# Norms of a two-block transformer: sums folded on VectorE, small steps moved there, columns spread by transposes, and the first four projections issued in a fixed order

## The chip, the cores and the metric

One NeuronCore of a Trainium2 chip runs the whole program. The metric is the device time of one execution in microseconds, given as the median of several executions. TensorE multiplies (its weight loads are listed apart, as PEld), VectorE (DVE) and ScalarE (ACT) work elementwise, GpSimd (POOL) does small steps, and SyncE (SP) issues the transfers.

## What is computed

The input is 256 tokens of 1024 features in float32. A first block has two layers (a retention and sparse-attention mixer, then a gated recurrent mixer, each followed by a gated feed-forward layer with 2816 inner features) with root-mean-square norms ahead of every part. A second block follows with a differential-attention layer and a chunked-attention layer, each again with a feed-forward layer, and here a layer norm stands *behind* every part:

```python
def layer_norm(x, g, b):
    mu = jnp.mean(xf, axis=-1, keepdims=True)
    var = jnp.mean(jnp.square(xf - mu), axis=-1, keepdims=True)
    y = (xf - mu) * lax.rsqrt(var + LN_EPS) * g + b
...
    x = layer_norm(DEEPNORM_ALPHA * x + mix, ln_g[l, 0], ln_b[l, 0])
    x = layer_norm(DEEPNORM_ALPHA * x + swiglu_2(x, ...), ln_g[l, 1], ln_b[l, 1])
```

There are thus five root-mean-square norms (four in the first block, one at its end) and four layer norms, the last of which ends the program.

## The kernel before, in words

Activations lie feature-major: 1024 features are eight slices of 128 partitions by 256 tokens, kept in four pair tiles (`State`). Every projection multiplies in three passes to keep float32 precision: both the weights and the activations are split into a high part on ScalarE and a low part on VectorE (`weights`, L235; `split`, L292), and `mm3` (L246) issues high by high, high by low and low by high for each of eight slices. One projection of 128 outputs, a *product* below, is thus 24 matmuls. Weights come by SyncE's queue, 512 KB at a time.

**The sums of a norm** run over partitions, so TensorE does them: `Stats` (L307) adds up squares (and, for a layer norm, the values too) over slices on VectorE and then multiplies each remaining 128 by 256 part by a constant column (L333). In the kernel before, slices 0 to 5 are folded into one part (`upto=4`) and slices 6 and 7 go to TensorE as they are: three parts, two token halves each, six matmuls a sum. The first norm of the program folds all eight (`upto=6`, L684). A float32 matmul shows in the profile as two records, so six matmuls are twelve records.

**The small steps** turn two sums per token into the reciprocal root. A layer norm copies the sums out of PSUM on VectorE (L507) and does five steps on GpSimd (L509, L510, L346, L349, L513). A root-mean-square norm does a copy on VectorE (L361) and two steps on GpSimd (L348, L349). `spread` (L352) then multiplies a broadcast column by the identity (L355), so that each token's number stands on all 128 partitions, and one copy takes that out of PSUM (L366 on VectorE, L517 on ScalarE).

**A layer norm defers its division.** `Norm` (L482) computes z = ALPHA times the earlier stream plus the mixer's output (L490), scales it by the gain on ScalarE (L493), splits it (L295, L296) and lets the next projections run on the result before the norm is known: `project` (L534) issues a product into a PSUM bank and only then, on VectorE, corrects it by the spread reciprocal root and mean (L541, L543, L544). Norm 0 stands behind the first attention layer's output projection, Norm 1 behind the first feed-forward layer, Norm 2 behind the second attention layer, and `last_norm` (L547) behind the last feed-forward layer. Behind Norm 0 and Norm 2 the first four products may use four banks (three of `pa`, one of `tr`); behind Norm 1 only the three of `pa`.

**The order of the work** is set by a planner at build time. It simulates the engines and, on each engine, takes what is ready, the earlier in the program first. What it decides is then each engine's fixed order. An order-only edge (`tc.issue_after(x)`) puts what follows behind instruction `x` on the same engine's queue, without waiting for `x` to finish.

Of the kernel before, what the change touches and what calls it, by code (L numbers as in the profile page):

```python
# [16 lines left out]
S = 256  # L17
# [151 lines left out]
def _model(es, tc, I, out):  # L169
# [12 lines left out]
    class State:  # L182
        def __init__(self):
            self.t = [None] * 4
# [61 lines left out]
    def mm3(ps, hi, lo, k, h, first, last):  # L246
        a, b = hi[:, k * 128:k * 128 + 128], lo[:, k * 128:k * 128 + 128]
        T.matmul(ps, a, h[0], start=first, stop=False, skip_group_check=True)  # L248
        T.matmul(ps, a, h[1], start=False, stop=False, skip_group_check=True)  # L249
        T.matmul(ps, b, h[0], start=False, stop=last, skip_group_check=True)  # L250

# [55 lines left out]
    class Stats:  # L307
        def __init__(self, cols, tag, upto=4):
            self.cols, self.tag, self.upto, self.ps = cols, tag, upto, None
            self.first, self.acc, self.parts = {}, {}, [[] for c in cols]  # L310

        def add(self, i, src, d, n):
            if d == 0:
                self.first[i] = src
            elif d == 2:
                self.acc[i] = sp.tile([128, 2, S], F32, tag="acc", name="acc")
                V.tensor_tensor(out=self.acc[i], in0=self.first[i], in1=src, op=ALU.add)
            elif d <= self.upto:
                a = self.acc[i]
                V.tensor_tensor(out=a, in0=a, in1=src, op=ALU.add)  # L320
                if d == self.upto:
                    V.tensor_tensor(out=a[:, 0], in0=a[:, 0], in1=a[:, 1], op=ALU.add)
                    self.parts[i].append(a[:, 0])
            else:
                self.parts[i] += [src[:, j] for j in range(n)]

        def total(self, i, last=True):
            start = self.ps is None
            if start:
                self.ps = att(self.tag, (128, 2 * len(self.cols)))  # L330
            for k, p in enumerate(self.parts[i]):
                for t in range(2):
                    T.matmul(self.ps[:, 2 * i + t:2 * i + t + 1], p[:, t * 128:t * 128 + 128], self.cols[i],  # L333
                             start=start and k + t == 0, stop=last and k == len(self.parts[i]) - 1,
                             skip_group_check=True)
            self.parts[i] = []

    def square(src, n):
# [4 lines left out]
    def rpow(v, n, eps, floor=False):  # L343
        r = sp.tile([128, n], F32, tag="rp", name="rp", bufs=6)
        if floor:
            G.tensor_scalar(out=r, in0=v, scalar1=0.0, scalar2=eps, op0=ALU.max, op1=ALU.add)  # L346
        else:
            G.tensor_scalar(out=r, in0=v, scalar1=eps, scalar2=None, op0=ALU.add)  # L348
        G.tensor_tensor(out=r, in0=r, in1=mhalf[:, :n], op=ALU.pow)  # L349
        return r  # L350

    def spread(cols, ps):  # L352
        for i, c in enumerate(cols):
            for t in range(2):
                T.matmul(ps[:, i, t * 128:t * 128 + 128], c[:, t:t + 1].to_broadcast([128, 128]), ident,  # L355
                         start=True, stop=True)

    def rms_stats(stats, eps=1e-6):
        stats.total(0)
        v = sp.tile([128, 2], F32, tag="v2", name="v2", bufs=6)  # L360
        V.tensor_copy(v, stats.ps)  # L361
        rt = rpow(v, 2, eps)
        pb = att("po", (128, 1, S))
        spread([rt], pb)
        rb = sp.tile([128, S], F32, tag="rb", name="rb", bufs=2)
        V.tensor_copy(rb, pb[:, 0])  # L366
        return rb, rt

    def prep(X, goff, upto=4):
        stats, H = Stats((mcol,), "po", upto), []  # L370
        for d in range(8):
# [110 lines left out]
    class Norm:  # L482
        def __init__(self, src, gen, idx, tag, tags=()):
            self.gcol, self.bcol = V_LNG + idx * 8, V_LNB + idx * 8
            self.zg, self.HD = State(), []
            self.tags = list(tags)
# [46 lines left out]

        def project(self, w, f):  # L534
            tag, shape = self.tags.pop(0) if self.tags else "pa", [128, S + 2]
            ps = pa.tile(shape, F32, tag="pa", name="pd") if tag == "pa" else att(tag, shape)
            hi, lo = weights(w[f], 1024)
            for k in range(8):
                mm3(ps, hi, lo, k, self.HD[k], k == 0, k == 7)
            c = sp.tile([128, 2], F32, tag="dc", name="dc", bufs=4)  # L540
# [41 lines left out]
    def transpose_to(ps, src):  # L582
        T.transpose(ps, src, ident)  # L583
# [85 lines left out]
    def even_mixer(X):  # L669
# [13 lines left out]
        nc.scalar.dma_start(out=ident, in_=I["const"][:, 0:128])  # L683
        H, rb, rt = prep(X, V_MIX, 6)  # L684
        w1 = [big("w1").rearrange("p a b -> p (a b)") for i in range(4)]
# [474 lines left out]

    FOUR = ("pa", "pa", "pa", "tr")

# [4 lines left out]
    src.Y, gen = diff_mixer(X)  # L1167
    ln = Norm(src, gen, 0, "po", FOUR)
    ln = Norm(ln, ffn(ln, I["v1_0"], I["v3_0"], I["v2_0"], None), 1, 'po')

# [86 lines left out]

    ln = Norm(ln, chunk_mixer(ln), 2, "po", FOUR)
    last_norm(ln, ffn(ln, I["v1_1"], I["v3_1"], I["v2_1"], None), 3)


# [14 lines left out]
```

## Time and profile before

| | before |
|---|---|
| median of 3 runs (lowest to highest) | 1310.83 us (1310.12 to 1310.96) |
| the profiled execution: its own time | 1310.83 us |
| the profiled execution: span from first to last instruction | 1309.0 us |
| TensorE busy | 1289.9 us, 99% of the span |
| VectorE busy | 939.7 us, 72% |
| ScalarE busy | 708.2 us, 54% |
| GpSimd busy | 44.3 us, 3% |
| mean granted TensorE clock | 0.996 of full |

In the rows below, times are microseconds from the span's start. A TensorE record's length is its way through the array, and records overlap, so a stream of matmuls costs the distance from one start to the next and not the length shown. An entry in square brackets is how long the engine was idle before the instruction and what it waited for.

### The profile page before, as it was taken

The numbers are of one execution on the slowest core, as the hardware profiler recorded it, in microseconds if no ns is written. First come the engines' busy times: TensorE is split into PE (matmuls) and PEld (weight loads), VectorE is DVE, ScalarE is ACT, GpSimd is POOL, SyncE is SP. The second block draws the span as 40 slices with busy tenths as digits, with TensorE's granted clock in tenths as the row PEclk, the third lists the DMA queues.
The fourth block names the chain that finished last, engine by engine and source line by source line (L and its number), as shares of the span: only waits on it lengthen the run. The fifth ranks groups of instructions, "written<-read, shape, count | busy, mean of one in ns | idle before, by whom it ended". The sixth has DMA issues, their size and how long they took to land.

```text
span 1309.0 us, 27435 instructions
## 1 busy us (share of the span) xinstructions
PE 1289.9 (99%) x11112; PEld 1246.4 (95%) x11112; DVE 939.7 (72%) x1753; ACT 708.2 (54%) x1182; POOL 44.3 (3%) x97
## 2 busy tenths in 40 slices
PE   8999999999999999999999999999999999999997
PEld 7989999999989999999999899999999889999997
DVE  7886774645888667565678959777779757968675
ACT  6675654444644455443468856544456556554443
POOL 1000000000000000000000111000000000000000
PEclk9999999999999999999999999999999999999998
DMA  9623555554643346555555345465654544655550
GB/s 303 189 91 106 202 193 189 182 187 145 205 158 123 125 163 205 191 182 191 159 172 178 113 146 169 156 210 162 190 173 167 171 136 129 213 187 182 187 152 33
DMA packets 65358, 219.69 MB, mean 168 GB/s; under 512 B 7504, under 2 KB 7888, under 8 KB 65232
## 3 DMA queue, kind: packets, MB, share of 16 engines
q1 hardware_dynamic: 64944, 217.82, 51.1%
q8 instruction: 87, 1.43, 0.4%
q14 instruction: 39, 0.32, 0.1%
q10 hardware_dynamic: 288, 0.12, 0.0%
HBM read 216.86 MB, written 1.05 MB: 166 GB/s over the span
## 4 chain that ended last, share of the span: by engine, by line
PE 96%; DMA 1%; DVE 1%; ACT 1%; issue 0%; SPq 0%; POOL 0%; ACTq 0%; DVEq 0%
PE pa L249 13%; PE pa L248 13%; PE pa L250 13%; PE pd L249 7%; PE pd L248 7%; PE pd L250 7%; PE s L248 4%; PE s L250 4%; PE s L249 4%; PE tr L248 3%; PE tr L249 3%; PE tr L250 3%; PE pv L284 2%; PE pv L285 2%; PE pv L286 2%; PE tr L583 1%
## 5 line engine op out<-in xcount | busy, mean ns | idle before, releaser
L240 ACT ACTIVATE hi<-raw 128x1024 fp32r<-128x1024 f32 (+2 forms) x421 | 424.5, 1018 | 487.7 <-PE pa L249 166.6
L243 DVE TENSOR_TENSOR lo<-raw,hi 128x1024 fp32r<-128x1024 f32 (+2 forms) x421 | 490.7, 1173 | 251.2 <-ACT hi L240 244.6
L249 PE MATMUL pa<-hl,hi 128*128 128x256 f32 x1424 | 402.6, 284 | 0.2 <-issue 0.2
L248 PE MATMUL pa<-hh,hi 128*128 128x256 f32 x1424 | 401.0, 284 | 0.3 <-DVE x L479 0.2
L250 PE MATMUL pa<-hh,lo 128*128 128x256 f32 x1424 | 401.1, 283 | 0.0
L249 PEld LDWEIGHTS pa<-hl,hi 128*128 128x128 f32 x1424 | 268.6, 189 | 2.7 <-issue 0.9
L250 PEld LDWEIGHTS pa<-hh,lo 128*128 128x128 f32 x1424 | 268.5, 189 | 1.5 <-issue 0.5
L248 PEld LDWEIGHTS pa<-hh,hi 128*128 128x128 f32 x1424 | 267.0, 188 | 2.6 <-issue 0.5
L249 PE MATMUL pd<-hl,hi 128*128 128x258 f32 x752 | 212.7, 284 | 0.0
L250 PE MATMUL pd<-hh,lo 128*128 128x258 f32 x752 | 212.7, 283 | 0.0
L248 PE MATMUL pd<-hh,hi 128*128 128x258 f32 x752 | 211.0, 283 | 1.4 <-DVE y L543 1.4
L248 PEld LDWEIGHTS pd<-hh,hi 128*128 128x128 f32 x752 | 141.7, 190 | 1.7 <-DVE y L543 1.6
L249 PEld LDWEIGHTS pd<-hl,hi 128*128 128x128 f32 x752 | 142.5, 190 | 0.0
L250 PEld LDWEIGHTS pd<-hh,lo 128*128 128x128 f32 x752 | 142.2, 189 | 0.2
L250 PE MATMUL s<-gh,lo 128*128 128x256 f32 x352 | 97.6, 279 | 0.0
L249 PE MATMUL s<-gl,hi 128*128 128x256 f32 x352 | 97.6, 279 | 0.0
L248 PE MATMUL s<-gh,hi 128*128 128x256 f32 x352 | 95.8, 280 | 0.0
L248 PE MATMUL tr<-gh,hi 128*128 128x256 f32 x264 | 73.8, 280 | 0.0
L249 PE MATMUL tr<-gl,hi 128*128 128x256 f32 x264 | 73.7, 279 | 0.0
L250 PE MATMUL tr<-gh,lo 128*128 128x256 f32 x264 | 73.7, 279 | 0.0
L250 PEld LDWEIGHTS s<-gh,lo 128*128 128x128 f32 x352 | 66.1, 188 | 0.0
L249 PEld LDWEIGHTS s<-gl,hi 128*128 128x128 f32 x352 | 66.0, 187 | 0.0
(353 smaller groups left out, 1914.3 us busy)
## 6 DMA issues: line engine op xcount, KB each, us to landing
raw<-w SPq DMA_DIRECT2D x120, 512.0 KB, 3.8
raw<-v SPq DMA_DIRECT2D x120, 512.0 KB, 3.9
raw<-w_e SPq DMA_DIRECT2D x19, 512.0 KB, 5.8
raw<-w_aqk SPq DMA_DIRECT2D x16, 512.0 KB, 3.8
raw<-w SPq DMA_DIRECT2D x16, 384.0 KB, 3.1
raw<-v SPq DMA_DIRECT2D x16, 384.0 KB, 3.1
raw<-w_of SPq DMA_DIRECT2D x8, 512.0 KB, 3.3
raw<-w_oq SPq DMA_DIRECT2D x8, 512.0 KB, 3.9
```

The lines of the kernel that those rows point to most:

```text
L240: A.activation(hi, raw, AF.Copy)
L243: V.tensor_tensor(out=lo, in0=raw, in1=hi.bitcast(F32), op=ALU.subtract)
L248: T.matmul(ps, a, h[0], start=first, stop=False, skip_group_check=True)
L249: T.matmul(ps, a, h[1], start=False, stop=False, skip_group_check=True)
L250: T.matmul(ps, b, h[0], start=False, stop=last, skip_group_check=True)
L284: T.matmul(ps[t], xh, a, start=k == 0, stop=False)
L285: T.matmul(ps[t], xh, b, start=False, stop=False)
L286: T.matmul(ps[t], xl, a, start=False, stop=k == 7)
L583: T.transpose(ps, src, ident)
```

## The change

Sums are folded further on VectorE: the root-mean-square norms fold all eight slices, a layer norm folds all eight of its values and the first seven of its squares, and the last norm the first seven of both. The small steps except the power move from GpSimd to VectorE. `spread` uses TensorE's transpose in place of a multiplication by the identity. In a layer norm the squares are taken ahead of the gain and the split, and the first four products behind it are issued inside `Norm`: the first as it comes, the other three queued behind the last matmul of the sums, and the spread queued behind the last matmul of the third product. Behind Norm 1, too, the fourth product now uses a bank of `tr`. The core of the diff (the rest passes the new arguments on, or returns the instruction just issued):

```diff
     class Stats:
-        def __init__(self, cols, tag, upto=4):
+        def __init__(self, cols, tag, folded):
...
-            elif d <= self.upto:
+            elif d < self.folded[i]:
                 a = self.acc[i]
-                V.tensor_tensor(out=a, in0=a, in1=src, op=ALU.add)
-                if d == self.upto:
+                at = a[:, d % 2:d % 2 + n]
+                V.tensor_tensor(out=at, in0=at, in1=src, op=ALU.add)
+                if d + n == self.folded[i]:
                     V.tensor_tensor(out=a[:, 0], in0=a[:, 0], in1=a[:, 1], op=ALU.add)
                     self.parts[i].append(a[:, 0])
...
     def rpow(v, n, eps, floor=False):
         r = sp.tile([128, n], F32, tag="rp", name="rp", bufs=6)
         if floor:
-            G.tensor_scalar(out=r, in0=v, scalar1=0.0, scalar2=eps, op0=ALU.max, op1=ALU.add)
+            V.tensor_scalar(out=r, in0=v, scalar1=0.0, scalar2=eps, op0=ALU.max, op1=ALU.add)
         else:
-            G.tensor_scalar(out=r, in0=v, scalar1=eps, scalar2=None, op0=ALU.add)
+            V.tensor_scalar(out=r, in0=v, scalar1=eps, scalar2=None, op0=ALU.add)
         G.tensor_tensor(out=r, in0=r, in1=mhalf[:, :n], op=ALU.pow)
...
     def spread(cols, ps):
-                T.matmul(ps[:, i, t * 128:t * 128 + 128], c[:, t:t + 1].to_broadcast([128, 128]), ident,
-                         start=True, stop=True)
+                transpose_to(ps[:, i, t * 128:t * 128 + 128], c[:, t:t + 1].to_broadcast([128, 128]))

     def rms_stats(stats, eps=1e-6):
         stats.total(0)
-        v = sp.tile([128, 2], F32, tag="v2", name="v2", bufs=6)
-        V.tensor_copy(v, stats.ps)
-        rt = rpow(v, 2, eps)
+        rt = rpow(stats.ps, 2, eps)
...
     class Norm:
-            stats = Stats((ncol, mcol), tag)
+            stats = Stats((ncol, mcol), "po", (8, 7))
             for d, n, ps in gen:
                 z = ...
+                stats.add(1, square(z, n), d, n)
...
                 stats.add(0, z, d, n)
-                stats.add(1, square(z, n), d, n)
             stats.total(0)
-            stats.total(1)
+            summed = stats.total(1)
...
-            G.tensor_tensor(out=v, in0=st[:, 0:2], in1=st[:, 0:2], op=ALU.mult)
-            G.tensor_tensor(out=v, in0=st[:, 2:4], in1=v, op=ALU.subtract)
+            V.tensor_tensor(out=v, in0=st[:, 0:2], in1=st[:, 0:2], op=ALU.mult)
+            V.tensor_tensor(out=v, in0=st[:, 2:4], in1=v, op=ALU.subtract)
             r = rpow(v, 2, 1e-5, True)
             mr = sp.tile([128, 2], F32, tag="mr", name="mr")
-            G.tensor_tensor(out=mr, in0=st[:, 0:2], in1=r, op=ALU.mult)
-            pb = att("po", (128, 2, S))
-            spread([r, mr], pb)
+            V.tensor_tensor(out=mr, in0=st[:, 0:2], in1=r, op=ALU.mult)
+            self.ahead = {}
+            for i, (w, f, bk) in enumerate(ahead):
+                with tc.issue_after(summed.ins) if i else nullcontext():
+                    self.ahead[w.tensor.name, f] = self.product(w, f, bk)
+                if i == 2:
+                    with tc.issue_after(self.latest.ins):
+                        pb = att("po", (128, 2, S))
+                        spread([r, mr], pb)
...
     def last_norm(src, gen, idx):
-        zs, qs = Stats((ncol,), "sc"), Stats((mcol,), "sc")
+        zs, qs = Stats((ncol,), "sc", (7,)), Stats((mcol,), "sc", (7,))
...
-            if d == 4:
+            if d == 6:
                 zs.total(0, False)
                 qs.total(0, False)
...
-    ln = Norm(ln, ffn(ln, I["v1_0"], I["v3_0"], I["v2_0"], None), 1, 'po')
+    ln = Norm(ln, ffn(ln, I["v1_0"], I["v3_0"], I["v2_0"], None), 1,
+              first_four((I["w_bk"], 0), (I["w_bk"], 1), (I["w_bq"], 0), (I["w_bq"], 1)))
```

`product` is the part of `project` that issues the 24 matmuls; `project` takes a product that was issued ahead, or issues one itself.

## Rows read from the trace of the kernel before

**Rows 1.** The page: span, busy time of two engines, and the chain that ended last.

```profile
span 1309.0 us, 27435 instructions
...
PE 1289.9 (99%) x11112; PEld 1246.4 (95%) x11112; DVE 939.7 (72%) x1753; ACT 708.2 (54%) x1182; POOL 44.3 (3%) x97
...
PE 96%; DMA 1%; DVE 1%; ACT 1%; issue 0%; SPq 0%; POOL 0%; ACTq 0%; DVEq 0%
```

**Rows 2.** Waits of TensorE, longest in total first: us in total, times, longest.

```profile
PE pd L248 <- DVE y L543: 1.4, 1, 1.4
...
PE pa L355 <- POOL rp L349: 0.8, 1, 0.8
```

**Rows 3.** Whole span, instructions of L333, then of L355 alone: PE busy, records.

```profile
0.00:1309.00 1309.00, 17.19 (x148) 17.56 (x148) 1.00 0.52 168
...
0.00:1309.00 1309.00, 8.38 (x52) 7.11 (x52) 1.00 0.52 168
```

**Rows 4.** Chain that ended last, in order of time: start, us, what.

```profile
67.03 0.66 PE tr L583 x6
...
153.97 1.23 PE po L333 x12
...
799.39 0.89 PE po L355 x8
```

**Rows 5.** Timeline of TensorE behind Norm 0: start, length, line, operation.

```profile
786.93 0.52 PE L248 MATMUL pd<-hh,hi 128*128 128x258 f32 x3
...
792.96 0.50 PE L333 MATMUL po<-mcol,acc 128*128 128x1 f32 x4
793.33 1.03 PE L333 MATMUL po<-mcol,sq 128*128 128x1 f32 x8
...
802.06 0.28 PE L248 MATMUL pd<-hh,hi 128*128 128x258 f32 x1
802.18 0.28 PE L249 MATMUL pd<-hl,hi 128*128 128x258 f32 x1
```

**Rows 6.** Timeline of VectorE around Norm 0, the same columns.

```profile
788.44 0.41 DVE L490 SCALAR_TENSOR_TENSOR z<-x,s 128x256 f32<-128x256 f32 x1
788.77 0.42 DVE L322 TENSOR_TENSOR acc<-acc 128x256 f32<-128x256 f32 x1
789.11 0.69 DVE L320 TENSOR_TENSOR acc<-acc,sq 128x512 f32<-128x512 f32 x1
789.71 0.68 DVE L296 TENSOR_TENSOR hl<-x,hh 128x512 fp32r<-128x512 f32 x1
790.32 0.41 DVE L322 TENSOR_TENSOR acc<-acc 128x256 f32<-128x256 f32 x1
790.65 1.36 DVE L296 TENSOR_TENSOR hl<-x,hh 128x512 fp32r<-128x512 f32 x3
```

**Rows 7.** Timeline behind Norm 1: VectorE's last splits, TensorE's fourth product.

```profile
983.24 0.76 DVE L296 TENSOR_TENSOR hl<-x,hh 128x256 fp32r<-128x256 f32 x2
...
994.37 0.39 PE L248 MATMUL pd<-hh,hi 128*128 128x258 f32 x1 [1.36 <-DVE y L543]
```

**Rows 8.** Timeline of VectorE and GpSimd in the last norm.

```profile
1296.27 0.42 DVE L552 SCALAR_TENSOR_TENSOR x<-x,po 128x256 f32<-128x256 f32 x1 [1.16 <-PE po L250]
1298.39 0.16 DVE L562 COPY m<-s 128x2 f32<-128x2 f32 x1 [1.70 <-PE s L333]
...
1299.39 2.48 DVE L570 TENSOR_TENSOR x<-x,pa 128x512 f32<-128x512 f32 x4 [0.38 <-PE pa L355]
1301.79 2.47 DVE L573 TENSOR_TENSOR x<-x,pa 128x512 f32<-128x512 f32 x4
...
1299.41 0.71 POOL L349 TENSOR_TENSOR rp<-rp,mhalf 128x2 f32<-128x2 f32 x1
```

**Rows 9.** Stretches: length, busy PE, PEld, DVE, ACT, POOL, granted clock, DMA, GB/s.

```profile
991.50:994.50 3.00, 1.64 (x12) 1.21 (x11) 2.50 (x5) 2.48 (x4) 0.66 (x2) 1.00 0.96 322
...
1295.90:1309.00 13.10, 4.68 (x35) 4.19 (x34) 6.50 (x14) 3.47 (x7) 0.93 (x2) 0.64 0.21 80
```

More of the change, by code (lines that the diff above doesn't have):

```diff
@@ L249, in mm3 @@
         T.matmul(ps, a, h[1], start=False, stop=False, skip_group_check=True)
-        T.matmul(ps, b, h[0], start=False, stop=last, skip_group_check=True)
+        return T.matmul(ps, b, h[0], start=False, stop=last, skip_group_check=True)
     PB = {"s0": 1, "s1": 1, "tr": 2, "po": 1}
@@ L307, in _model @@
     class Stats:
[L308 to L309 removed]
+        def __init__(self, cols, tag, folded):
+            self.cols, self.tag, self.folded, self.ps = cols, tag, folded, None
             self.first, self.acc, self.parts = {}, {}, [[] for c in cols]
@@ L332, in total @@
                 for t in range(2):
-                    T.matmul(self.ps[:, 2 * i + t:2 * i + t + 1], p[:, t * 128:t * 128 + 128], self.cols[i],
-                             start=start and k + t == 0, stop=last and k == len(self.parts[i]) - 1,
-                             skip_group_check=True)
+                    ins = T.matmul(self.ps[:, 2 * i + t:2 * i + t + 1], p[:, t * 128:t * 128 + 128], self.cols[i],
+                                   start=start and k + t == 0, stop=last and k == len(self.parts[i]) - 1,
+                                   skip_group_check=True)
             self.parts[i] = []
+            return ins
     def square(src, n):
@@ L367, in rms_stats, with prep @@
         return rb, rt
-    def prep(X, goff, upto=4):
-        stats, H = Stats((mcol,), "po", upto), []
+    def prep(X, goff):
+        stats, H = Stats((mcol,), "po", (8,)), []
         for d in range(8):
@@ L482, in _model, with __init__ @@
     class Norm:
-        def __init__(self, src, gen, idx, tag, tags=()):
+        def __init__(self, src, gen, idx, ahead):
             self.gcol, self.bcol = V_LNG + idx * 8, V_LNB + idx * 8
             self.zg, self.HD = State(), []
-            self.tags = list(tags)
-            stats = Stats((ncol, mcol), tag)
+            stats = Stats((ncol, mcol), "po", (8, 7))
             for d, n, ps in gen:
@@ L532, in normalize, with product, project @@
             return self.H
-        def project(self, w, f):
-            tag, shape = self.tags.pop(0) if self.tags else "pa", [128, S + 2]
-            ps = pa.tile(shape, F32, tag="pa", name="pd") if tag == "pa" else att(tag, shape)
+        def product(self, w, f, tag="pa"):
+            ps = pa.tile([128, S + 2], F32, tag="pa", name="pd") if tag == "pa" else att(tag, (128, S + 2))
             hi, lo = weights(w[f], 1024)
             for k in range(8):
-                mm3(ps, hi, lo, k, self.HD[k], k == 0, k == 7)
+                self.latest = mm3(ps, hi, lo, k, self.HD[k], k == 0, k == 7)
+            return ps
+        def project(self, w, f):
+            ps = self.ahead.pop((w.tensor.name, f), None)
+            if ps is None:
+                ps = self.product(w, f)
             c = sp.tile([128, 2], F32, tag="dc", name="dc", bufs=4)
@@ L683, in even_mixer @@
         nc.scalar.dma_start(out=ident, in_=I["const"][:, 0:128])
-        H, rb, rt = prep(X, V_MIX, 6)
+        H, rb, rt = prep(X, V_MIX)
         w1 = [big("w1").rearrange("p a b -> p (a b)") for i in range(4)]
@@ L1159, in diff_mixer, with first_four, gates_of @@
         return X, out_proj((I["w_ao"], I["w_aol"]), M)
-    FOUR = ("pa", "pa", "pa", "tr")
+    def first_four(*wf):
+        return [(w, f, bk) for (w, f), bk in zip(wf, ("pa", "pa", "pa", "tr"))]
+    def gates_of(w1, w3):
+        return first_four((w1, 0), (w3, 0), (w1, 1), (w3, 1))
     class Source:
@@ L1167, in _model @@
     src.Y, gen = diff_mixer(X)
-    ln = Norm(src, gen, 0, "po", FOUR)
-    ln = Norm(ln, ffn(ln, I["v1_0"], I["v3_0"], I["v2_0"], None), 1, 'po')
+    ln = Norm(src, gen, 0, gates_of(I["v1_0"], I["v3_0"]))
+    ln = Norm(ln, ffn(ln, I["v1_0"], I["v3_0"], I["v2_0"], None), 1,
+              first_four((I["w_bk"], 0), (I["w_bk"], 1), (I["w_bq"], 0), (I["w_bq"], 1)))
     def chunk_mixer(ln):
@@ L1256, in chunk_mixer @@
         return out_proj((I["w_bo"], I["w_bol"]), M)
-    ln = Norm(ln, chunk_mixer(ln), 2, "po", FOUR)
+    ln = Norm(ln, chunk_mixer(ln), 2, gates_of(I["v1_1"], I["v3_1"]))
     last_norm(ln, ffn(ln, I["v1_1"], I["v3_1"], I["v2_1"], None), 3)
```

## The prediction

> **What bounds the kernel now.** I read the page first, for the engine that sets the time. TensorE is busy for 99% of the span, and 96% of the chain that ended last is TensorE's own queue [rows 1]. Busy time alone would prove little, since records overlap, so I went on to the waits: the longest that TensorE shows behind a norm are 1.4 us for a correction on VectorE (L543) and 0.8 us for GpSimd's power step [rows 2]. So nearly every TensorE record that goes is time that goes, and nearly nothing that GpSimd saves is, except at these two places. The question is what TensorE loses where its order becomes stricter. For that I read the timelines around each norm.
>
> **What TensorE no longer does.** The sums (L333) are 148 records, the spreads (L355) 52 [rows 3]. By the code a root-mean-square norm falls from three parts to one (12 records to 4; four norms, as the first was so already), a layer norm from 24 records to 12 (one part for the values, two for the squares; three norms), the last norm from 24 to 16. That is 32 + 36 + 8 = 76 records. Their price is the distance between starts: 1.23 us for 12, or 0.103 us each [rows 4]. For the spread the price is 0.89 us for 8 records, and a transpose, which shows as one record where the float32 product shows as two, ran at 0.66 us for 6 [rows 4]: 0.11 us a record in both. So a spread halves, 26 records go.
>
> The Trainium skill (TensorE: Matmul & The Clock Gate, Part 4: PE-mode transpose) gives about 275 ns for a transpose inside a kernel, which a stream of six in 0.66 us does not bear out as a price. By the page's figure as the price, 26 transposes would cost an estimated 7.2 us against 5.8 us for the 52 records, a loss of 1.4 us where I count a gain of 2.9 us.
>
> **The root-mean-square norms.** Around them TensorE streams projections that need no norm, so the records come straight off: 32 x 0.103 = 3.3 us, and five spreads of two records less, 10 x 0.11 = 1.1 us. Together 4.4 us. The fold costs VectorE one more add of 512 columns, 0.69 us as at L320 [rows 6], per norm, and the sums become ready that much later; the copy and one of the two GpSimd steps leave the chain behind. Both lie beside the projections. If that cover were gone it would cost 0.7 us a norm, 2.8 us in all.
>
> **Norm 0 and Norm 2: the strict order.** Before, TensorE goes from the output projection at 786.93 us to the fifth product at 802.06 us, 15.13 us [rows 5]: 96 matmuls at 0.12 us (the two starts at the end of rows 5) are 11.5 us, sums 2.5 us, spread 0.9 us. It fills the time in which VectorE still makes the sums and the splits with matmuls of three or four products. After the change only the first product, 24 matmuls, may run ahead of the sums; 12 fewer sum records (1.23 us) and 4 fewer of the spread (0.44 us) stand against an empty TensorE. How long it is empty VectorE decides. It works without pause to 792.01 us, when the last low part is done, and its fold of the squares stands at 790.32 to 790.73 us [rows 6]. It gets three more adds of 256 columns, each 0.33 us (the distance from 788.44 to 788.77 us [rows 6]), 1.0 us. If the sums go ahead of the last splits they are ready at 790.7 + 1.0 = 791.7 us, if behind them at 793.0 us. Eight to twelve records follow (0.8 to 1.2 us): the second product starts between 792.5 and 794.2 us. Then come 72 matmuls (8.6 us), the spread (0.44 us), the changes between kinds of matmul (0.2 us; 15.13 us leave 0.26 us over the terms above) and up to six matmuls of the first product whose slices were late (0.7 us). The fifth product would start between 801.8 and 804.2 us: a gain of 0.3 us to a loss of 2.1 us. I take a loss of 0.5 us, as the last value at 788.44 us [rows 6] went ahead of older splits, nearer the early end. Two such norms: +1.0 us, from -0.6 to +4.2 us.
>
> The small steps are hidden here. The copy and four steps on VectorE at 0.16 us, as L562, and the power at 0.71 us [rows 8] are some 1.5 us, some 3 us with hand-overs, and a low part of weights or two may stand in front; the second and third product cover 5.8 us. If they did not, the spread would hold the fourth product, which is queued behind nothing but the sums.
>
> **Norm 1.** Before, the fourth product had no bank, waited for the correction of the first and started at 994.37 us after 1.36 us idle [rows 7]; at 24 x 0.12 us it ends at 997.2 us. Afterwards it has a bank of its own and the spread goes ahead of it. VectorE's last splits end at 984.0 us [rows 7]; with 1.0 us of adds and 1.2 us of sums the second product starts by 986.2 us at the latest, by about 983.5 us if the sums go first. With 8.6 + 0.44 + 0.2 us the fourth ends between 992.8 and 995.5 us, a gain of 1.7 to 4.4 us. I take 3.0 us, which is also the wait (1.36 us) plus the records (1.23 + 0.44 us). Late next is the fifth product's bank: copy of the spread, copy of a column and correction are some 1.5 us, under the fourth product's 2.9 us.
>
> **The last norm** is all in the open. The last value is ready at 1296.69 us, its sum is read at 1298.39 us, and the four adds that use it start at 1299.39 us [rows 8], all 24 records lying between. Now 8 records can go as early as TensorE is free, and 4 follow the last value: read at about 1297.5 us, then 2 records of spread instead of 4. The adds start about 1.0 us sooner. They last 2.4 us, and the reciprocal root must be there when they end: one GpSimd step less, and the power, at 1299.41 us before [rows 8], moves up with the sums. I take 1.0 us, from 0.3 us (the power arrives late) to 1.2 us.
>
> **The sum.** -4.4 + 1.0 - 3.0 - 1.0 = -7.4 us. The profiled execution took 1310.83 us (its span and 1.83 us around it), just the median: 1303.4 us.
>
> **Rivals.**
> 1. *Starved, at full clock.* The planner places the last values and folds behind the splits at all three norms. Norm 0 and 2 then cost 2.1 us each, Norm 1 gains only 1.7 us, and the last norm 0.3 us: -4.4 + 4.2 - 1.7 - 0.3 = -2.2 us, 1308.6 us, no change by the measure of 0.2% (2.6 us, about what a measurement of this kernel can tell). For it: VectorE has no gap there. Against: the squares now come first in the program.
> 2. *Starved, and the clock falls: slower.* Behind the sums of Norm 0 and Norm 2 TensorE has stood partly empty for some 3 us and run one-column matmuls. If the granted clock drops there from 2.4 to 1.2 GHz, the 72 matmuls that follow take 8.6 us more each time: 1303.4 + 17.3 = 1320.7 us. It decides as soon as the granted clock in these stretches is under about 0.8. For it: in the last 13.1 us, after the sum records and with waits between, the mean grant is 0.64. Against: across the wait of 1.36 us at Norm 1 it stayed at 1.00 [rows 9]. The Trainium skill (TensorE: Matmul & The Clock Gate, Why this matters for your kernels) warns of idle gaps between bursts of matmuls for just this; the trace bears it out only at the end of the program.
> 3. *More comes off.* The sums are early everywhere, Norm 0 and 2 gain 0.3 us each, Norm 1 4.4 us, the end 1.2 us: -4.4 - 0.6 - 4.4 - 1.2 = -10.6 us, 1300.2 us.
> 4. *The transposes do not halve the spread.* Should a transpose of a broadcast column show two records, 2.9 us stay: 1306.3 us. Against: the others show one.
>
> Over all of these, the planner may order other stages differently once the norms are shorter; the few waits that TensorE has bound that to a microsecond or two in either direction.
>
> **How the numbers follow.** Forecast (1303.4 us, by itself 1301 to 1306 us) 0.58; more comes off 0.14; transposes do not halve 0.06; starved 0.12; clock falls 0.07; something else of the planner's making, either sign, 0.03. The range leaves out most of the clock case and a little at each end: 1299.5 to 1308.5 us. Faster by over 0.2% (under 1308.2 us): 0.58 + 0.14 + 0.06 + a third of the starved case, 0.82. Same: 0.10. Slower: the clock case and a rest, 0.08.
>
> **What would show it.** Right: L333 with 72 records and L355 gone, 26 transposes more at L583; no GpSimd step but the power in the norms; behind Norm 0 and 2 a TensorE gap of 1 to 3 us ahead of the sums, with granted clock 1.00; no wait of the fourth product behind Norm 1; the last adds 1 us nearer to the last matmul. Wrong: a granted clock under 1.00 there; sums that wait for VectorE beyond 793 us on the old clock of Norm 0; a spread that holds TensorE; new waits in stages that the change does not touch.

## The result, and the profile after

The change makes the kernel slower: 1317.57 us is the median of nine runs (1313.17 to 1323.25) beside 1310.96 us before, a ratio of 1.0054 (95% interval 1.0044 to 1.0064). One of the nine runs of the kernel before took 1784.54 us and stands outside that ratio; the other eight lie between 1310.04 and 1311.48 us. The profiled execution took 1317.5 us, 6.6 us more of span than before.

The page of the kernel after: span, busy time (us, share, instructions), and the chain that ended last.

```profile
span 1315.6 us, 27222 instructions
...
PE 1287.7 (98%) x11010; PEld 1242.4 (94%) x11010; DVE 947.6 (72%) x1787; ACT 707.8 (54%) x1182; POOL 32.9 (3%) x73
...
PE 94%; DVE 3%; ACT 1%; issue 1%; DMA 0%; POOL 0%; ACTq 0%; SPq 0%; DVEq 0%
```

TensorE has 102 records fewer than in [rows 1], the 76 and 26 that were counted, yet VectorE's share of the chain rose from 1% to 3%. The waits of TensorE after (us in total, times, longest) say where:

```profile
PE pd L249 <- DVE hl L296: 5.3, 6, 1.5
PE pd L248 <- DVE y L552: 2.2, 1, 2.2
...
PE pv L286 <- DVE hl L296: 1.0, 1, 1.0
```

The 1.4 us of [rows 2], at Norm 1, is gone, but at Norm 2 a product now waits 2.2 us for a correction (L552, which was L543). New are six waits of a product behind a layer norm for the low part of its own input (`hl`), and one of the chunk mixer's value projection (`pv`), also for a low part. Below, a wait in square brackets is idle time; "between starts" means the distance from one matmul's start to the next, which is 0.12 us where nothing is waited for. Behind Norm 0 the timeline of TensorE, as [rows 5], is now this (start, length, line, operation, idle before and its releaser):

```profile
782.23 0.36 PE L248 MATMUL pd<-hh,hi 128*128 128x258 f32 x1
783.52 0.36 PE L249 MATMUL pd<-hl,hi 128*128 128x258 f32 x1 [0.93 <-POOL hh L496]
...
784.20 0.28 PE L248 MATMUL pd<-hh,hi 128*128 128x258 f32 x1
785.99 0.36 PE L249 MATMUL pd<-hl,hi 128*128 128x258 f32 x1 [1.50 <-DVE hl L296]
...
788.54 0.58 PE L334 MATMUL po<-ncol,acc 128*128 128x1 f32 x4
...
789.87 0.36 PE L248 MATMUL pd<-hh,hi 128*128 128x258 f32 x1
...
795.75 0.38 PE L592 MATMUL po<-ident,rp 128*128 128x128 f32 x2
795.97 0.38 PE L592 MATMUL po<-ident,mr 128*128 128x128 f32 x2
...
799.08 0.28 PE L248 MATMUL pd<-hh,hi 128*128 128x258 f32 x1
```

The first product starts 4.70 us earlier than in [rows 5], its sums are halved, and the spread takes two records in place of four for each of its two numbers per token. But from 782.23 to the second product at 789.87 us TensorE has only 24 matmuls and 12 sum records, and stands still twice inside the first product (1.29 and 1.79 us between starts). VectorE, as [rows 6], explains why (same columns):

```profile
781.49 0.68 DVE L317 TENSOR_TENSOR acc<-sq 128x512 f32<-128x512 f32 x1
782.09 0.68 DVE L317 TENSOR_TENSOR acc<-z 128x512 f32<-128x512 f32 x1
782.69 0.68 DVE L296 TENSOR_TENSOR hl<-x,hh 128x512 fp32r<-128x512 f32 x1
783.29 0.68 DVE L321 TENSOR_TENSOR acc<-acc,z 128x512 f32<-128x512 f32 x1
783.89 0.68 DVE L321 TENSOR_TENSOR acc<-acc,sq 128x512 f32<-128x512 f32 x1
784.50 0.74 DVE L488 SCALAR_TENSOR_TENSOR z<-x,s 128x256 f32<-128x256 f32 x2
785.16 1.28 DVE L296 TENSOR_TENSOR hl<-x,hh 128x512 fp32r<-128x512 f32 x2
```

Two adds stand ahead of one low part and two adds and two values ahead of the next; TensorE's matmuls at 783.52 and 785.99 us start as these low parts end. The first of the two is put down to a small copy on GpSimd, which ends within 0.05 us of the low part; the same wait behind Norm 2, below, has the low part alone as its releaser. Behind Norm 2 the same happens, and then something more. TensorE there:

```profile
1104.54 0.35 PE L248 MATMUL pd<-hh,hi 128*128 128x258 f32 x1
1105.83 0.36 PE L249 MATMUL pd<-hl,hi 128*128 128x258 f32 x1 [0.94 <-DVE hl L296]
...
1108.30 0.36 PE L249 MATMUL pd<-hl,hi 128*128 128x258 f32 x1 [1.51 <-DVE hl L296]
...
1121.96 0.38 PE L592 MATMUL po<-ident,rp 128*128 128x128 f32 x2
...
1124.74 0.39 PE L248 MATMUL pd<-hh,hi 128*128 128x258 f32 x1 [2.19 <-DVE y L552]
```

and VectorE's small steps between them:

```profile
1113.38 0.16 DVE L505 COPY st<-po 128x4 f32<-128x4 f32 x1
1113.45 2.36 DVE L243 TENSOR_TENSOR lo<-raw,hi 128x1024 fp32r<-128x1024 f32 x2
...
1117.35 1.22 DVE L243 TENSOR_TENSOR lo<-raw,hi 128x1024 fp32r<-128x1024 f32 x1 [0.74 <-ACT hi L240]
1118.49 0.16 DVE L348 TENSOR_SCALAR rp<-v 128x2 f32<-128x2 f32 x1
...
1119.47 0.16 DVE L511 TENSOR_TENSOR mr<-st,rp 128x2 f32<-128x2 f32 x1
```

The copy of the sums and four steps of 0.16 us each take from 1113.38 to 1119.63 us, since low parts of weights stand between them. One of these low parts is itself late: with the next small step behind it in the queue, VectorE stands idle for 0.74 us until ScalarE has made the high part. The planner then put the spread behind the fourth product, and the fifth waits for a bank. Last, the granted clock, in the stretches in which it is lower (columns as [rows 9]):

```profile
982.60:989.40 6.80, 6.80 (x34) 6.80 (x33) 5.51 (x11) 2.92 (x3) 0.70 (x1) 0.50 0.62 201
...
1013.30:1016.70 3.40, 3.40 (x9) 2.66 (x9) 3.40 (x14) 1.87 (x5) 0.00 (x0) 0.51 0.81 287
...
1108.90:1112.30 3.40, 3.40 (x18) 3.40 (x18) 3.40 (x10) 3.40 (x6) 0.00 (x0) 0.50 0.00 0
...
1126.00:1129.40 3.40, 3.40 (x18) 3.40 (x17) 3.40 (x8) 0.94 (x3) 0.00 (x0) 0.50 0.32 120
```

That is 17.0 us at 1.2 in place of 2.4 GHz with TensorE busy throughout, so 8.5 us lost. They stand behind Norm 1, in the chunk mixer, and twice behind Norm 2; before, no stretch between the start and the last norm shows a lower clock. The second stretch behind Norm 2 and the one in the chunk mixer follow waits of 2.46 and of 0.9 and 1.4 us between starts.

The 6.6 us put together from starts of matmuls, after against before: up to Norm 0's first product -4.70; from there to the fifth product 16.85 in place of 15.13 us, +1.72; on to Norm 2's first product (Norm 1 and the chunk mixer) +4.03; Norm 2's first to fifth product 20.20 in place of 15.12 us, +5.08; on to the last weight matmul +1.64; from there to the end -1.18. Without the 8.5 us of the clock, -1.9 us would remain.

### The profile page after: what moved, and what is told of

It reads as the page before. It is cut to its first block, busy times and chain, and to the rows that moved or that the text cites. A ratio compares the mean times of both kernels' runs of the same rounds, so it can differ in the third digit from the quotient of the medians.

```text
span 1315.6 us, 27222 instructions
## 1 busy us (share of the span) xinstructions
PE 1287.7 (98%) x11010; PEld 1242.4 (94%) x11010; DVE 947.6 (72%) x1787; ACT 707.8 (54%) x1182; POOL 32.9 (3%) x73
## 3 DMA queue, kind: packets, MB, share of 16 engines
HBM read 216.86 MB, written 1.05 MB: 166 GB/s over the span
## 4 chain that ended last, share of the span: by engine, by line
PE 94%; DVE 3%; ACT 1%; issue 1%; DMA 0%; POOL 0%; ACTq 0%; SPq 0%; DVEq 0%
PE pa L248 13%; PE pa L249 13%; PE pa L250 13%; PE pd L248 7%; PE pd L249 7%; PE pd L250 7%; PE s L248 4%; PE s L249 4%; PE s L250 4%; PE tr L249 3%; PE tr L248 3%; PE tr L250 3%; PE pv L284 2%; PE pv L286 2%; PE pv L285 2%; PE tr L592 1%
## 5 line engine op out<-in xcount | busy, mean ns | idle before, releaser
L248 PE MATMUL pd<-hh,hi 128*128 128x258 f32 x744 | 213.7, 287 | 2.3 <-DVE y L552 2.2
```

## The experiments

All were timed in five rounds against the kernel before (medians 1310.64 and 1310.77 us), with five to eleven runs of each kernel. Unless another kernel is named, the base is the kernel before for the first two and the changed kernel for the rest.

**The fixed order alone**, with the fourth bank that it needs behind Norm 1:

```diff
+            for i, (w, f, bk) in enumerate(ahead):
+                with tc.issue_after(summed.ins) if i else nullcontext():
+                    self.ahead[w.tensor.name, f] = self.product(w, f, bk)
...
```

> The kernel before, with the fixed order of the first four products and the fourth bank behind Norm 1 alone; sums, small steps and spreads as before. Theory A: slower than the kernel before, 1315 to 1325 us, with runs that differ by up to 10 us and a granted clock of 0.5 in stretches behind the layer norms. Theory B: within 2.6 us of before, as VectorE has its old load: 1308 to 1313 us.

Measured: 1321.06 us (1317.80 to 1322.76), 1.0076 (1.0064 to 1.0088). The order alone costs more than the whole change, as theory A had it. TensorE stands 1.05 and 0.51 us between starts in the first product behind Norm 0 and again behind Norm 2, and the clock is at half from 792.0 to 798.8 and from 1112.8 to 1119.7 us. With VectorE's old load these two waits are not for low parts but for a high part on ScalarE and for the fold of the values.

**The layer norms' small steps alone** on VectorE:

```diff
-            G.tensor_tensor(out=v, in0=st[:, 0:2], in1=st[:, 0:2], op=ALU.mult)
+            V.tensor_tensor(out=v, in0=st[:, 0:2], in1=st[:, 0:2], op=ALU.mult)
...
```

> The kernel before with nothing but the four small steps of a layer norm (and one of the last norm) moved from GpSimd to VectorE. Theory C (the small steps, each waiting for the one before, get a low part of weights of some 1.2 us queued between them on VectorE; the spread comes late, holds TensorE, and the clock falls): 1313 to 1320 us, waits of TensorE at L355 behind Norm 0 and Norm 2, granted clock 0.5 for some microseconds behind them. Theory A (only the strict order costs) and theory B (only the added adds and the squares first cost): 1309 to 1312 us.

Measured: 1316.35 us (1314.98 to 1318.28), 1.0044 (1.0030 to 1.0058), so theory C by the time. But the wait did not come at the spread, where the theory had it: it came at the fifth product, 2.10 us between starts behind Norm 0 and Norm 2 alike, and the clock fell to half behind the first alone, for 3.4 us. VectorE around Norm 0 in this kernel, then TensorE's fifth product:

```profile
794.19 0.16 DVE L507 COPY st<-po 128x4 f32<-128x4 f32 x1
794.26 1.22 DVE L243 TENSOR_TENSOR lo<-raw,hi 128x1024 fp32r<-128x1024 f32 x1
...
799.63 0.16 DVE L513 TENSOR_TENSOR mr<-st,rp 128x2 f32<-128x2 f32 x1 [0.52 <-POOL rp L349]
...
803.74 0.36 PE L248 MATMUL pd<-hh,hi 128*128 128x258 f32 x1 [1.82 <-DVE y L543]
```

5.60 us from the copy of the sums to the last step; with the steps on GpSimd (the fastest of the kernels without the order, below) 3.60 us, although each of the four steps that move is longer there. Of the 2.0 us between the two, 1.0 us is the power step, which is on GpSimd in both and took 1.71 us in the first and 0.72 us in the second:

```profile
789.91 1.10 POOL L507 TENSOR_TENSOR v<-st 128x2 f32<-128x2 f32 x1 [6.76 <-DVE st L505]
...
792.50 0.78 POOL L511 TENSOR_TENSOR mr<-st,rp 128x2 f32<-128x2 f32 x1
```

The Trainium skill (GPSIMD Engine Reference, its opening) calls GpSimd the wrong choice for ordinary elementwise arithmetic, VectorE being about twice as fast. By the single step the rows agree (0.16 against 0.20 to 1.10 us); by the chain they don't: here the idle queue beat the fast one with 1.2 us instructions in it.

**The rest without the ordered products**: folds, steps on VectorE, transposes, squares first; products issued as before, and only three banks behind Norm 1. Then the same **with the fourth bank** behind Norm 1:

```diff
-            for i, (w, f, bk) in enumerate(ahead):
...
+            pb = att("po", (128, 2, S))
+            spread([r, mr], pb)
+            self.tags = list(ahead)
...
-    ln = Norm(ln, ffn(ln, I["v1_0"], I["v3_0"], I["v2_0"], None), 1,
-              first_four((I["w_bk"], 0), (I["w_bk"], 1), (I["w_bq"], 0), (I["w_bq"], 1)))
+    ln = Norm(ln, ffn(ln, I["v1_0"], I["v3_0"], I["v2_0"], None), 1, ())
```

With the fourth bank the last argument is `FOUR` in place of `()`.

> Only the folds, the small steps on VectorE, the transposes and the squares first; products issued in project as before, three banks behind Norm 1. Theory A: the gains of the sums and spreads alone, 4.4 us at the five root-mean-square norms, about 1 us at the end, 1 to 2 us a layer norm: 1302 to 1306 us. Theory B: 1309 to 1314 us.

> As the kernel with the sums, steps and transposes only, and a fourth bank for the fourth product behind Norm 1. Theory A: another 1 to 3 us off that kernel, as the wait of 1.36 us that the kernel before had there goes: 1300 to 1304 us. Theory B: no better than the kernel before by more than 1 us.

Measured: 1317.67 us (1315.85 to 1319.69), 1.0054 (1.0042 to 1.0066); with the bank 1313.92 us (1313.54 to 1316.17), 1.0027 (1.0016 to 1.0038). The bank is worth 3.75 us: without it TensorE waits 3.6 us for the power step behind Norm 1 alone. But the change is slower than before with no forced order in it as well, so the order is not the only cause. The first time lies above the ranges of both theories; the second is as theory B had it.

**The changed kernel without the edge** behind the sums, the spread still placed by hand:

```diff
-                with tc.issue_after(summed.ins) if i else nullcontext():
-                    self.ahead[w.tensor.name, f] = self.product(w, f, bk)
+                self.ahead[w.tensor.name, f] = self.product(w, f, bk)
```

> The changed kernel, with the first four products still issued inside the norm, but without the edge that queues the second to fourth behind the sums. Theory A (the strict order starves TensorE: it waits for the first product's low parts with nothing else to run, and the clock falls): the waits of 1.2 to 1.8 us in the first product go, the granted clock stays at 1.00 behind all three norms, 1301 to 1306 us, and the runs agree within 0.3%. Theory B (VectorE is overloaded: three more adds a norm and the squares first make the low parts late for every product): the waits stay in some form, 1310 to 1316 us.

Measured: 1314.74 us (1313.89 to 1316.40), 1.0032 (1.0020 to 1.0044). The waits at the first product shrink to one of 0.98 us between starts, and new ones of 1.4 and 1.1 us stand at the spread, for `rp` and `mr`, the small steps' results. 2.8 us come back, which is theory B's range and not theory A's (1301 to 1306 us).

**The small steps back on GpSimd**, once without the forced order (base: the version with the bank), once in the changed kernel:

```diff
-            V.tensor_tensor(out=v, in0=st[:, 0:2], in1=st[:, 0:2], op=ALU.mult)
+            G.tensor_tensor(out=v, in0=st[:, 0:2], in1=st[:, 0:2], op=ALU.mult)
...
```

> Folds, transposes and squares first as in the change, four banks behind Norm 1, no fixed order, and the small steps of a layer norm back on GpSimd (those of the other norms stay on VectorE). Theory C: the waits at the spread (1.4 and 1.1 us behind Norm 0 and 2) go, 1303 to 1308 us with the clock at 1.00; waits of about 1 us at the first product's second slice stay. Theory B: still 1311 us or more.

> The changed kernel with the small steps of a layer norm back on GpSimd, the fixed order kept. Theory A: the waits of 1.3 and 1.8 us in the first product stay, with the falls of the clock that follow, 1312 to 1320 us; the wait of 2.46 us behind Norm 2 goes, as the spread is ready behind the third product. Theory C alone (the order costs nothing once the steps are in time): 1303 to 1308 us.

Measured: 1310.73 us (1308.03 to 1312.43), 0.9998 (0.9990 to 1.0007), and with the order 1312.83 us (1310.01 to 1317.42), 1.0018 (1.0007 to 1.0028). The steps give back 3.2 us without and 4.7 us with the order. With the order it came out as theory A had it: 1.29 and 1.80 us between starts stay in the first product at Norm 0 and Norm 2. Without the order theory C's range (1303 to 1308 us) failed: what stays is 0.97 us in the first product for a low part, 0.67 us at the spread for the power step, and 1.79 to 2.67 us at the fifth product behind each of the three norms, where a bank is waited for.

**Squares behind the split and six columns folded, as before** (base: the version without order, steps on GpSimd); then **only the squares moved back**, with the longer folds kept:

```diff
-            stats = Stats((ncol, mcol), "po", (8, 7))
+            stats = Stats((ncol, mcol), "po", (6, 6))
...
-                stats.add(1, square(z, n), d, n)
...
                 stats.add(0, z, d, n)
+                stats.add(1, square(z, n), d, n)
```

> The same, with the squares behind the split again and a layer norm's folds as before (slices 0 to 5), so that what is left of the change is the folds of the other norms, the transposes and the fourth bank behind Norm 1. Theories A, B and C agree: 1302 to 1306 us, no wait of TensorE over 0.5 us behind Norm 0, 1 and 2. If this is not faster than the kernel before, all three lack something.

> The kernel with the small steps on GpSimd, products in no forced order and a fourth bank at Norm 1 (1310.7 us), with the squares again behind the split; seven and eight columns still folded. The version that also folds six again took 1305.8. Theory A (squares ahead of the split hold up the low parts): most of the 4.9 us comes back, 1305.5 to 1307.5, and the first product behind Norm 0 has no wait of about 1 us. Theory B (the longer folds make the sums and all behind them late): 1309 to 1311, the sums still stand behind more than 60 products' matmuls at Norm 0, and a wait of 1.5 us or more stays behind the spread.

Measured: 1305.79 us (1304.32 to 1306.29), 0.9958 (0.9946 to 0.9971), faster than before, with no wait over 0.5 us behind Norm 0 and Norm 2 but one of 2.55 us between starts behind Norm 1, which the theories did not have; with the longer folds 1309.25 us (1308.48 to 1310.54), 0.9989 (0.9980 to 0.9998). So of the 4.9 us the squares' place holds 1.5 and the folds 3.5 us; theory B on the folds was the nearer, though the waits that it named were smaller (0.88 us idle behind the spread of Norm 0) and the first product's wait stayed (1.27 us idle, for a low part behind the adds), which theory A had laid on the squares. The sums show how the folds work. With folds of eight and seven, then of six, squares behind the split in both, TensorE's first records of the sums behind Norm 0 (the first products start at 781.99 and 782.11 us):

```profile
789.50 0.50 PE L334 MATMUL po<-ncol,acc 128*128 128x1 f32 x4
789.87 0.58 PE L334 MATMUL po<-mcol,acc 128*128 128x1 f32 x4
```

```profile
784.63 0.50 PE L334 MATMUL po<-ncol,acc 128*128 128x1 f32 x4
...
788.15 0.50 PE L334 MATMUL po<-mcol,acc 128*128 128x1 f32 x4
```

Folding more saves an estimated 1.2 us of records (12 at 0.103 us) and lets the sums start 4.9 us (values) and 1.7 us (squares) later, behind matmuls that would otherwise have covered the small steps; the copy that opens these steps and needs both sums comes 1.7 us later (791.40 and 789.68 us). Norm 0 takes 15.86 us from the first to the fifth product with the longer folds and 14.66 us with six, 0.47 us less than before.

**The fixed order on top of this fastest version** (the diff is against the changed kernel, whose order is kept):

```diff
-            stats = Stats((ncol, mcol), "po", (8, 7))
+            stats = Stats((ncol, mcol), "po", (6, 6))
...
-                stats.add(1, square(z, n), d, n)
...
                 stats.add(0, z, d, n)
+                stats.add(1, square(z, n), d, n)
...
-            V.tensor_tensor(out=mr, in0=st[:, 0:2], in1=r, op=ALU.mult)
+            G.tensor_tensor(out=mr, in0=st[:, 0:2], in1=r, op=ALU.mult)
```

> The changed kernel with its fixed order of the first four products kept, but the small steps on GpSimd, the squares behind the split and six columns folded as before. Beside 1305.8 us without the fixed order this is the order alone. Theory A (the order itself costs, since the first product alone stands behind the sums' chain and the low parts): TensorE waits 1 us or more in the first product or ahead of the second at Norm 0 and Norm 2, 1310 to 1316 us. Theory B (the order only cost because its values and low parts came late, which the other edits mend): 1304 to 1307 us and no wait above 1 us behind Norm 0 and Norm 2.

Measured: 1312.51 us (1310.45 to 1315.41), 1.0016 (1.0007 to 1.0025): 6.7 us for the order alone, so theory A. TensorE in the first product behind Norm 0, and the stretch after it:

```profile
784.29 0.39 PE L248 MATMUL pd<-hh,hi 128*128 128x258 f32 x1 [0.77 <-ACT hh L295]
784.80 0.61 PE L334 MATMUL po<-ncol,acc 128*128 128x1 f32 x4
```

```profile
786.60:793.40 6.80, 6.80 (x34) 6.80 (x33) 4.69 (x8) 4.03 (x5) 1.54 (x5) 0.50 0.46 145
```

The waits are now short, 1.05 and 0.51 us between starts. The clock falls all the same: from the first to the fifth product Norm 0 takes 19.34 us where it takes 14.66 us without the order, and 3.4 of these 4.7 us are the half clock of that stretch. Norm 2 has the same again (19.36 and 14.69 us), and the chunk mixer a further 3.4 us at half clock: 8.5 of the 9.8 us between the two profiled executions are clock.

**The waits filled**, in the changed kernel: 27 idle matmuls per layer norm, between the first product and the second, whose results the second product overwrites:

```diff
+            if after == 1:
+                for i in range(27):
+                    T.matmul(ps, self.hi0[:, 0:128], self.HD[0][0], start=True, stop=True, skip_group_check=True)
```

> The changed kernel with 27 more matmuls per layer norm between the first product and the second. They multiply the first product's weights, which are there, into the second product's bank, which that product then overwrites; they stand where TensorE waits for the sums, and add at most 27 x 0.11 = 3.0 us per layer norm where it would not have waited. Theory (the waits of 1 to 2 us behind the layer norms cost twice, once as waits and once by the granted clock that falls to half behind them): the second cost goes behind the norms, the granted clock is 1.00 behind Norm 0 and Norm 2, the runs lie within 3 us of one another, and the median is 1308 to 1314 us in spite of the added work. Rival (the waits alone cost): nothing comes back, 1318 to 1322 us.

Measured: 1314.29 us (1312.60 to 1316.13), 1.0027 (1.0016 to 1.0039). Added work made the kernel 3.3 us faster, though the median lies 0.3 us outside the theory's range, the runs lie 3.5 us apart and the clock was not 1.00 throughout. In the profile the fill stands where the waits stood, and no half clock follows it; but the planner now put the spread behind the fourth product at Norm 0 too, and behind that wait the clock fell at both norms:

```profile
783.01 3.35 PE L541 MATMUL pd<-hh,hi 128*128 128x258 f32 x26
...
801.99 0.39 PE L248 MATMUL pd<-hh,hi 128*128 128x258 f32 x1 [2.19 <-DVE y L557]
```

```profile
803.10:806.50 3.40, 3.40 (x18) 3.40 (x18) 3.08 (x7) 0.01 (x1) 0.00 (x0) 0.50 0.36 130
```

The rival, by which nothing comes back, failed. The stretches at half clock last 6.8 us in place of 17.0, which is worth 5.1 us, and the profiled execution is 1.4 us shorter (1316.13 and 1317.5 us), so the fill and the moved spread took back some 3.7 us. The other runs bear it out: the mean grant is 0.995 or more in all six, 0.994 or less in all nine of the changed kernel. So a wait can cost twice, once in itself and once by the clock.

**One edge added to the fastest version**: behind Norm 1 the fourth product queues behind the spread.

```diff
+            with tc.issue_after(self.spread.ins) if self.spread and tag == "tr" else nullcontext():
+                ps = self.product(w, f, tag)
```

> The fastest version so far (1305.8 us: the norms' folds, transposes and fourth bank of the change, its layer norms' small steps on GpSimd, squares behind the split, six folded, no forced order) with one edge: behind Norm 1 the fourth product waits until the spread has been issued. Theory (there the spread came 2.1 us after its values were ready because the fourth product went first, so that no bank was free and TensorE waited 2.55 us): the wait goes, 1303 to 1305 us. Rival (the spread goes ahead but its values are late, and TensorE waits for them instead): 1305 to 1308, with a wait of 1 us or more ahead of the spread.

Measured: 1302.84 us (1302.63 to 1303.08), 0.9939 (0.9926 to 0.9953), 7.8 us faster than before and the best of all. The fifth product behind Norm 1 in the version without the edge, then the spread with it, then the whole stretch between the start and the last norm:

```profile
991.96 0.39 PE L248 MATMUL pd<-hh,hi 128*128 128x258 f32 x1 [2.19 <-DVE y L545]
```

```profile
986.57 0.43 PE L589 MATMUL po<-ident,rp 128*128 128x128 f32 x2
987.19 0.43 PE L589 MATMUL po<-ident,mr 128*128 128x128 f32 x2 [0.20 <-POOL mr L512]
```

```profile
14.00:1293.00 1279.00, 1273.73 (x11017) 1230.73 (x11016) 929.74 (x1741) 693.99 (x1157) 35.95 (x77) 1.00 0.53 168
```

That is just under the theory's range; the rival's wait for values is there but is 0.2 us. The longest waits left between the start and the last norm are 0.63 and 1.40 us between starts in the chunk mixer (1004.85 and 1006.56 us); the clock stays at 1.00 and the runs lie within 0.45 us, where the changed kernel's lie within 10.

Each part's price, from pairs of kernels that differ in it alone:

| part | pairs (medians, us) | costs | at full clock |
|---|---|---|---|
| fixed order of the products | 1312.51 and 1305.79; 1312.83 and 1310.73; 1317.57 and 1314.74 (edge only); 1321.06 and 1310.8 (with the fourth bank) | 6.7; 2.1; 2.8; 10.3 | 1.2; -1.1; -1.5; 1.6 |
| layer norms' steps on VectorE | 1316.35 and 1310.8; 1313.92 and 1310.73; 1317.57 and 1312.83 | 5.6; 3.2; 4.7 | 3.6; 1.6; 1.3 |
| folds of eight and seven | 1309.25 and 1305.79 | 3.5 | 2.1 |
| squares ahead of the split | 1310.73 and 1309.25 | 1.5 | 2.4 |
| fourth bank behind Norm 1 | 1313.92 and 1317.67 | -3.8 | -1.1 |
| the rest: other norms' folds and steps, transposes, with the bank | 1305.79 and 1310.8 | -5.0 | -6.5 |

The last column is an estimate from one profiled execution of each kernel: the difference of their times, after half of what TensorE is busy at half clock between the start and the last norm is taken off each. By it the fixed order costs almost wholly through the clock, and the bank saves mostly by it; the steps on VectorE, the longer folds and the squares cost by waits too. The transposes are not what lowers the clock: the version with one edge spreads by them and its clock stays at 1.00, and the order alone spreads without them and its clock falls.

The costs don't add up to the change's: the parts share the same waits and the stretches of clock behind them.

## Why the prediction was wrong

**The root-mean-square norms: right.** -4.4 us forecast, -4.70 us measured up to Norm 0, of which some 0.4 us are shorter waits of the transposes in the differential attention (1.21 us idle in place of 0.77 and 0.84) and no record of a norm. The transposes halve the spread: two stand 0.22 us from the next two at 795.75 us, 0.11 us each. The 275 ns of the Trainium skill (TensorE: Matmul & The Clock Gate, Part 4: PE-mode transpose) are again no price per transpose in a stream.

**The last norm: right.** -1.0 us forecast, -1.18 us measured. VectorE, as [rows 8]: last value, its sum read, first add.

```profile
1304.05 0.42 DVE L561 SCALAR_TENSOR_TENSOR x<-x,po 128x256 f32<-128x256 f32 x1
1305.28 0.16 DVE L571 COPY m<-s 128x2 f32<-128x2 f32 x1 [0.81 <-PE s L334]
...
1306.01 2.47 DVE L579 TENSOR_TENSOR x<-x,pa 128x512 f32<-128x512 f32 x4
```

From value to add 1.96 us, where [rows 8] show 3.12.

**How the miss adds up.** The profiled execution took 6.6 us more of span where 7.4 us less was forecast, a miss of 14.0 us. The granted clock, which the sum put at nothing, is 8.5 us of it. At full clock Norm 2 is 2.9 us over its forecast (3.4 in place of 0.5 us), Norm 0 1.2 us, Norm 1 with the chunk mixer 1.9 us, and the rest 0.5 us under.

**Norm 0 and Norm 2, "I take a loss of 0.5 us" each: the step that failed first.** Norm 0 lost 1.72 us, inside the bounds given (-0.3 to +2.1); Norm 2 lost 5.08. The step asked when the sums would be ready and priced late slices of the first product at "up to six matmuls", 0.7 us of work. But the first product, which now stood alone, waited for them with nothing behind it to fill the time: 3.2 us over the pace of 0.12 us per matmul at Norm 0 (gaps of 1.29, 1.79 and 0.47 us). On the old clock the sums began at 793.2 us and the squares' last fold ended at 793.5, past the late end of 793.0. The second product started 7.64 us behind the first, where 5.6 to 7.3 was forecast; at Norm 2, with the clock at half on the way, 8.66 us. What the low parts stood behind were VectorE's adds, more of them than before and, with the squares first, earlier.

**"The small steps are hidden here": failed at Norm 2.** It was noted that "a low part of weights or two may stand in front". At Norm 2 they took 6.25 us in place of some 3, longer than the 5.8 us of cover. And the outcome was another than "the spread would hold the fourth product": the planner let the fourth go first, and the fifth waited 2.46 us between starts.

**Norm 1, -3.0 us.** The 1.36 us wait of [rows 7] went, and the bank is worth 3.75 us between two kernels, so the mechanism was there. But the second product started 7.14 us behind the first (984.43 and 977.29 us), where 983.5 to 986.2 us on the old clock meant 3.2 to 5.9 us (the earlier of these two times stands in the prediction without a sum): here too the first product waited for low parts (0.58 and 1.17 us between starts). First to fifth product took 18.77 us in place of 17.07, 3.4 us of it by the clock, so 1.7 us are gained at full clock, the low end of the forecast. The gain was given back by the clock: between Norm 0's fifth and Norm 2's first product the profile shows +4.03 us, of which half of 6.8 + 3.4 us, 5.1 us, is half clock. At full clock it would have been -1.1 us for Norm 1 and the chunk mixer together, in which the waits at `pv` (0.9 and 1.4 us between starts) are new. "New waits in stages that the change does not touch" was on the list of what would show it wrong; the bound of "a microsecond or two" for them held only at full clock.

**Rivals 1 and 2 came together.** Starved norms at full clock were put at 1308.6 us; the median less the profile's 8.5 us of clock is 1309.1. Rival 2 had the mechanism with the right sign, at 0.07. The argument against it, that the grant stayed at 1.00 across one wait of 1.36 us [rows 9], took one wait for all. Its price, 72 matmuls at half clock behind Norm 0 and Norm 2 (17.3 us), was too high: the stretches were shorter, and two of the four lay elsewhere. The nine runs confirm the size: the profile's grant averages 0.994 in the fastest and 0.986 in the slowest; 0.008 of some 1315 us is 10.5 us, and the runs lie 10.1 us apart. The Trainium skill (TensorE: Matmul & The Clock Gate, Why this matters for your kernels), which warns of idle gaps between bursts of matmuls, is borne out here in mid-kernel by waits of 1 to 2.5 us, shorter than the gaps that it names, though not behind each of them.

So the sum's gains were real (about 6 us outside the layer norms), and what failed was to put the clock at nothing, to price a wait once, and to price each norm as if its inputs came as before.

## What to carry to other kernels

Where TensorE streams work that needs no norm, fewer sum records and shorter spreads come straight off. Where the next products hang on the norm itself, the readiness of its inputs counts more than the records: look at what stands on the in-order queue ahead of each late input, and leave small dependent steps on an idle engine and the planner free to fill. Price a TensorE wait of 1 to 2.5 us there twice, as a wait and as a possible stretch at half clock.

## Not expected of the hardware

- The same waits had different outcomes. In the changed kernel the first product waits 1.29 and 1.79 us between starts at Norm 0 and at Norm 2; the grant stays at 1.00 behind the first and is 0.50 behind the second. A wait of 2.55 us (991.96 us in the version without the edge) left it at 1.00, waits of 1.05 and 0.51 us with sums behind them (784.29 us, order on the fastest version) brought it to 0.50. The chunk mixer's waits of 0.9 and 1.4 us were followed by half clock in the changed kernel, those of 0.63 and 1.40 us in the best version were not. The sums' one-column matmuls are not needed for a fall: behind Norm 2 of the changed kernel it comes at 1108.9 us, and the sums start at 1111.59 us. What tells the waits apart was not settled.
- The time that the lower clock costs varies between executions of one program: their times lie 10.1 us apart for the changed kernel, 0.45 us for the version without long waits behind the norms.
- Added matmuls made a kernel faster (1314.29 against 1317.57 us) by standing in its waits.
